# A linear head's norm ahead of its gate, output products taken head by head, and other buffers for half of the token-major weights

## The chip, the core and the metric

The kernel runs on one core of one Trainium2 chip. The core has a matrix engine (TensorE, PE in the rows), a vector engine (VectorE, DVE), an activation engine (ScalarE, ACT), GpSimd (POOL) and SyncE (SP), which issues most of the DMAs. Each engine works through its own list of instructions in a fixed order. The metric is the device time of one execution in microseconds (us), as the median of several runs.

## The reference

One sequence of 512 tokens with 1024 features passes two blocks, all in float32. The first block adds the output product of two mixers and then a gated feed-forward part (width 2816): eight heads of sparse attention (compressed, selected and window keys) and four linear heads with a decaying state. What matters here is the end of a linear head, and the output product over all heads:

```python
hgrn2_mixer(hq, hf, hi, hg, lb, o_gain):
    ...
    o = rms_norm(o, o_gain) * jax.nn.silu(hg.astype(f32)).reshape(B, T, H, dv)
    return o.reshape(B, T, H * dv)

first_block:
    mix = jnp.concatenate([o_nsa.astype(x.dtype), o_hgrn.astype(x.dtype)], axis=-1)
    x = x + mix @ w_out[l]
```

The second block has two layers. Each runs eight heads of stick-breaking attention and four heads of differential attention, adds their output product, and then a feed-forward part of width 4096 with a squared relu:

```python
        df_out = (rmsnorm(df_heads, subln_norm[l]) * (1.0 - lambda_init)).reshape(B, S, DF_WIDTH)
        mixed = jnp.concatenate([sb_out, df_out.astype(sb_out.dtype)], axis=-1)
        x = x + jnp.einsum('bse,ed->bsd', mixed, w_o[l])
```

A final norm follows.

## The kernel before

**Layout.** The sequence lies feature-major: eight tiles X of 128 features x 512 tokens. Every float32 factor of a large product is split into a high and a low part (`_h`, `_l`), and `mm3` (L407) makes one product of three matmuls: high x high, low x high, high x low. A matmul of 128 x 128 weights against 512 tokens is a "weight matmul" below. `load_w` (L383) brings a block of weights: SyncE issues a DMA into a `raw` buffer (3 of them), ScalarE casts the high part (L402) into a slot of the `hi` ring (2 slots), VectorE subtracts to get the low part (L403) in the `lo` ring (2 slots). With `tags` it uses other buffers in place of these rings (`kh`, `kl`), which otherwise hold keys and the compression weights.

**Products.** `gemm_fm` (not shown) makes feature-major results from loaded blocks. `gemm_nat` (L456) makes token-major ones, in four token blocks; it serves `whi` (the values `hv` of the linear heads) and `wvsw`. Results of these go to two PSUM banks (`mm`) and are read from there: `add_residual` adds them to X on VectorE (L504). `gemm_late` (L471) makes an output product of four heads of which the last are not ready when it starts: it waits until three heads are there, does their parts (k = 0, 1, 2) of two output tiles in `mm` banks and, when the scores are through, of more tiles in banks that the scores leave (`wl` in the names); then it waits for the fourth head, adds its part (k = 3) to each, emits them, and does the other tiles by `gemm_fm`. Before, it serves `w_out[0]` (the sparse heads) and, in each layer, `w_o2[l, 1]` (the differential heads). `w_out[1]` (the linear heads) goes through `gemm_fm`.

**Heads.** `hgrn_head` (L650) makes a linear head; its last product is `hpv`, whose squares ScalarE sums (`hsq`, L545). `head_out` (L547) makes the norm: the small `ho_v`, `nr_a`, `ho_rn` instructions on VectorE, the product `ho` (L564), four transposes `ho_t` on PE (L571), then the gate `hs` (L577) and the split in `ho_m_h` and `ho_m_l`. The gate of head h comes from the product `whg` (g0 to g3), through `gx`, `gsg` and `hs`. A differential head goes the same way without a gate: `dfo` (L1385), `dsq`, `do`, `do_t`, `do_m_h`.

**Order.** Several streams are written as Python generators: the linear heads, the setup and the units of the sparse attention, and the dense products (`dense1`). The table `ORDER1` (L39) is the order of the dense stream: i = whi, q = whqf, g = whg, n = sparse projections, v = wvsw, w = an output product, m = wait until that entry of `mix` (4 to 7 are the linear heads) is there. `_drive` (L178) calls the streams in turn and lets each go on when a planner (`Clock`, L73) with cost estimates for every engine and for DMAs (L141) thinks its inputs ready; `until` waits in this planning, not on the chip. Instructions written with `LOOKAHEAD` = 250 (L33) of priority, as the loads in `load_w`, are placed earlier. What comes out is one fixed list for each engine; on the chip an instruction waits in its list until its inputs and its buffer are free, and all behind it wait too.

The second block has its own streams and `ORDER2`; its differential attention and `gemm_late` run side by side there.

## Time and profile before

| what | value |
|---|---|
| median of 3 runs | 1999.33 us (1998.72 to 2000.38) |
| profiled execution: its own time | 1998.82 us |
| its span on the core | 1997.0 us |
| granted TensorE clock, mean | 0.996 of full |
| TensorE busy | 1964.2 us (98%) |
| VectorE busy | 1173.9 us (59%) |
| ScalarE busy | 885.3 us (44%) |
| GpSimd busy | 48.5 us (2%) |
| DMA | 168.65 MB, mean 84 GB/s |

The profiled execution is one run of the program; its span is the part between the first and the last instruction, 1.8 us shorter than its time. A row of a timeline gives the start and the duration of an instruction (or of several alike), then the line, the operation, what it writes and reads, and in brackets how long the engine had been idle before and what released it. Matmuls overlap their neighbours, so the step from one start to the next is shorter than the duration. In the names of rows buffer numbers are left out.

### The profile page before, as it was taken

To read this page: it belongs to the slowest core of one execution; us is meant where nothing else is said; L and a number is where in the kernel's file an instruction comes from. 1 tells how busy PE (TensorE), PEld (TensorE's weight loads), DVE (VectorE), ACT (ScalarE), POOL (GpSimd) and SP (SyncE) were. 2 spreads that over 40 slices of the span, in tenths; PEclk is the share of its full clock that TensorE was granted. 3 is DMA by queue.
4 is the path that set the end of the run, shared out by engine and by line. 5 is a ranking of instruction groups with operands and counts; after the bars stand their busy time and mean duration, and the time that the engine had idled before them with its cause. 6 is when DMAs were issued, how large, how long until landed. Compare 5 with 4: busy or idle time off the path is not lost.

```text
span 1997.0 us, 25958 instructions
## 1 busy us (share of the span) xinstructions
PE 1964.2 (98%) x10197; PEld 1602.2 (80%) x10197; DVE 1173.9 (59%) x2032; ACT 885.3 (44%) x1497; POOL 48.5 (2%) x92
## 2 busy tenths in 40 slices
PE   8999999999999999999999999999999999999998
PEld 7888876788888878787788888888887778888887
DVE  7687777644444455558764444447466864444445
ACT  7656445422222235677542233335487653222233
POOL 1000100000000000000000000000000000000000
PEclk9999999999999999999999999999999999999999
DMA  6222100222222222212222222223221212222222
GB/s 209 69 79 71 48 33 12 74 94 94 94 98 93 94 91 85 85 48 75 72 87 96 95 97 96 97 97 97 79 64 59 85 64 95 95 95 95 96 95 74
DMA packets 50922, 168.65 MB, mean 84 GB/s; under 512 B 5808, under 2 KB 8240, under 8 KB 50800
## 3 DMA queue, kind: packets, MB, share of 16 engines
q1 hardware_dynamic: 47680, 161.93, 24.6%
q0 software_dynamic: 2976, 4.98, 1.2%
q8 instruction: 81, 1.33, 0.3%
q14 instruction: 41, 0.34, 0.1%
q10 hardware_dynamic: 144, 0.07, 0.0%
HBM read 160.14 MB, written 2.10 MB: 81 GB/s over the span
## 4 chain that ended last, share of the span: by engine, by line
PE 89%; ACT 5%; DVE 4%; issue 2%; DMA 1%; SPq 0%; POOL 0%; DVEq 0%; ACTq 0%
PE L0wf_p L410 6%; PE L0wf_p L408 6%; PE L0wf_p L409 6%; PE L1wf_p L408 5%; PE L1wf_p L410 5%; PE L1wf_p L409 5%; PE wgu_p L408 4%; PE wgu_p L410 4%; PE wgu_p L409 4%; PE wdn_p L408 2%; PE wdn_p L410 2%; PE wdn_p L409 2%; PE hpl L710 1%; PE po L1076 1%; PE pt L1057 1%
## 5 line engine op out<-in xcount | busy, mean ns | idle before, releaser
L402 ACT CAST L0wf_h<-L0wf_r 128x1024 fp32r<-128x1024 f32 x64 | 67.3, 1051 | 226.2 <-PE L0wf_p L410 224.8
L402 ACT CAST L1wf_h<-L1wf_r 128x1024 fp32r<-128x1024 f32 x60 | 63.1, 1052 | 218.5 <-PE L1wf_p L410 217.3
L410 PE MATMUL wgu_p<-h_l,wgu_h 128*128 128x512 f32 x328 | 128.8, 393 | 0.0
L408 PE MATMUL wgu_p<-h_h,wgu_h 128*128 128x512 f32 x328 | 128.7, 392 | 0.0
L409 PE MATMUL wgu_p<-h_h,wgu_l 128*128 128x512 f32 x328 | 128.7, 392 | 0.0
L402 ACT CAST wgu_h<-wgu_r 128x1024 fp32r<-128x1024 f32 x44 | 46.2, 1051 | 161.7 <-issue 63.5
L408 PE MATMUL L0wf_p<-L0u_h,L0wf_h 128*128 128x512 f32 x256 | 100.7, 393 | 0.0
L409 PE MATMUL L0wf_p<-L0u_h,L0wf_l 128*128 128x512 f32 x256 | 100.4, 392 | 0.0
L410 PE MATMUL L0wf_p<-L0u_l,L0wf_h 128*128 128x512 f32 x256 | 99.4, 393 | 0.0
L410 PE MATMUL L0wf_p<-L0m_l,L0wf_h 128*128 128x512 f32 x240 | 94.2, 393 | 0.0
L410 PE MATMUL L1wf_p<-L1m_l,L1wf_h 128*128 128x512 f32 x240 | 94.2, 393 | 0.0
L408 PE MATMUL L1wf_p<-L1m_h,L1wf_h 128*128 128x512 f32 x240 | 94.2, 392 | 0.0
L408 PE MATMUL L0wf_p<-L0m_h,L0wf_h 128*128 128x512 f32 x240 | 94.2, 392 | 0.0
L409 PE MATMUL L0wf_p<-L0m_h,L0wf_l 128*128 128x512 f32 x240 | 94.1, 392 | 0.0
L409 PE MATMUL L1wf_p<-L1m_h,L1wf_l 128*128 128x512 f32 x240 | 94.1, 392 | 0.0
L403 DVE TENSOR_TENSOR L0wf_l<-L0wf_r,L0wf_h 128x1024 fp32r<-128x1024 f32 x64 | 78.4, 1225 | 23.4 <-ACT L0wf_h L402 23.4
L408 PE MATMUL L1wf_p<-L1u_h,L1wf_h 128*128 128x512 f32 x224 | 88.6, 395 | 0.0
L409 PE MATMUL L1wf_p<-L1u_h,L1wf_l 128*128 128x512 f32 x224 | 87.9, 392 | 0.0
L410 PE MATMUL L1wf_p<-L1u_l,L1wf_h 128*128 128x512 f32 x224 | 87.1, 394 | 0.0
L403 DVE TENSOR_TENSOR L1wf_l<-L1wf_r,L1wf_h 128x1024 fp32r<-128x1024 f32 x60 | 73.5, 1225 | 22.0 <-ACT L1wf_h L402 22.0
L504 DVE TENSOR_TENSOR X<-X,L0wf_p 128x512 f32<-128x512 f32 x64 | 43.9, 687 | 67.2 <-PE L0wf_p L410 67.2
L504 DVE TENSOR_TENSOR X<-X,L1wf_p 128x512 f32<-128x512 f32 x56 | 38.5, 688 | 67.3 <-PE L1wf_p L410 67.3
(904 smaller groups left out, 5383.8 us busy)
## 6 DMA issues: line engine op xcount, KB each, us to landing
L0wf_r<-w_ff SPq DMA_DIRECT2D x64, 512.0 KB, 3.3
L1wf_r<-w_ff SPq DMA_DIRECT2D x60, 512.0 KB, 3.3
wgu_r<-w_gu SPq DMA_DIRECT2D x44, 512.0 KB, 3.3
wdn_r<-w_dn SPq DMA_DIRECT2D x22, 512.0 KB, 3.3
wns_r<-w_nsa SPq DMA_DIRECT2D x8, 512.0 KB, 3.6
L0wsb_r<-w_sbqk SPq DMA_DIRECT2D x8, 512.0 KB, 3.3
L0wdf_r<-w_dfqk SPq DMA_DIRECT2D x8, 512.0 KB, 3.2
L1wsb_r<-w_sbqk SPq DMA_DIRECT2D x8, 512.0 KB, 3.3
```

The lines of the kernel that those rows point to most:

```text
L402: S.copy(hi[:, c], raw[:, c])
L403: V.tensor_tensor(lo[:, c], raw[:, c], _f(hi)[:, c], ALU.subtract)
L408: TE.matmul(ps, lh, rh, start=start, stop=False)
L409: TE.matmul(ps, ll, rh, start=False, stop=False)
L410: TE.matmul(ps, lh, rl, start=False, stop=stop)
L504: V.tensor_tensor(X[m], X[m], ps, ALU.add)
L710: TE.matmul(pl[:, b * 64 : (b + 1) * 64], ke[:, b * P : (b + 1) * P], qr[:, b * 64 : (b + 1) * 64], start=True, stop=True)
L1057: TE.transpose(pt[:, o + j * P : o + (j + 1) * P], p[g][:, j * P : (j + 1) * P], ident)
L1076: TE.matmul(po[g * 64 : (g + 1) * 64, 0:P], vsw[:, j, br * 128 + g * 64 : br * 128 + (g + 1) * 64], p[g][:, j * P : (j + 1) * P], start=Fa ...
```

## The change

It has five parts. `ORDER1` loses "m7", so that the dense stream goes on to w1 (`w_out[1]`) without a wait for the last linear head. The planner counts a DMA with 0.58 and 3.4 us in place of 0.5 and 3.0; this is an estimate used for ordering only. `gemm_nat` takes `tags` for its second half of weights, and whi passes ("kh", "kl"). `gemm_late` starts when the first head is there in place of three, goes over the heads outside and over its two tiles inside, waiting for each head, works with one block only where there are no scores to wait for, and now serves `w_out[1]` as well. And a linear head no longer waits for its gate before `hpv`: `head_out` takes the gate as a function and asks for it just before the transposes.

```diff
--- before.py
+++ after.py
@@ -36,7 +36,7 @@
 
 
 
-ORDER1 = "i0 q1 g0 n4 i1 q2 n6 g1 n0 m4 n7 n1 g2 m5 q3 n5 n2 n3 v0 g3 m7 w1"
+ORDER1 = "i0 q1 g0 n4 i1 q2 n6 g1 n0 m4 n7 n1 g2 m5 q3 n5 n2 n3 v0 g3 w1"
 
 
 ORDER2 = "q0 q2 s q1 d0 q3 v m3 d1 d2 d3 w0 w1 w3 w2"
@@ -138,7 +138,7 @@
                     if e != eng:
                         start = max(start, t + 0.06)
             if type(x).__name__ == "InstDMACopy":
-                end, eng = self.fit(eng, start, 0.5) + 3.0, "DMA"
+                end, eng = self.fit(eng, start, 0.58) + 3.4, "DMA"
             elif eng == "PE":
                 self.free["PE"] = start + cost
                 end = start + cost + 0.2
@@ -453,10 +453,11 @@
             G.dma_start(kh[o, g], kh[r, g])
         return kh, kl
 
-    def gemm_nat(src, h, emit, name):
+    def gemm_nat(src, h, emit, name, tags=None):
+
 
         cols = src.shape[3]
-        w = [load_w(src[hf], f"{name}_{hf}") for hf in range(2)]
+        w = [load_w(src[hf], f"{name}_{hf}", tags if hf else None) for hf in range(2)]
         for tb in range(NB):
             ps = bank("mm", f"{name}_p{tb}")[:, :cols]
             t = slice(tb * P, (tb + 1) * P)
@@ -474,27 +475,31 @@
 
         tiles = []
         cols = src.shape[3]
-        yield from until(lambda: all(x is not None for x in hs[:3]))
+        yield from until(lambda: hs[0] is not None)
         loaded = [load_w(src[b], f"{name}_{b}") for b in range(2)]
-        for b in range(2):
-            wh, wl = loaded[b]
+        for b in range(1 if scored is None else 2):
+            wh, wl = loaded.pop(0)
             if b == 1:
                 yield from until(scored)
                 loaded = [load_w(src[2], f"{name}_2", ("kh", "kl"))]
                 banks = spare_banks()
+            new = []
             for m in range(cols // P):
-                ps = bank("mm", f"{name}_p{b}_{m}") if b == 0 else banks[m]
                 c = slice(m * P, (m + 1) * P)
-                tiles.append((b * (cols // P) + m, ps, wh[:, 3, c], wl[:, 3, c]))
-                for k in range(3):
-                    mm3(ps, wh[:, k, c], wl[:, k, c], hs[k][0], hs[k][1], k == 0, False)
+                new.append((b * (cols // P) + m, bank("mm", f"{name}_p{b}_{m}") if b == 0 else banks[m], wh[:, :, c], wl[:, :, c]))
+            for k in range(3):
+                yield from until(lambda: hs[k] is not None)
+                for m, ps, wh, wl in new:
+                    mm3(ps, wh[:, k], wl[:, k], hs[k][0], hs[k][1], k == 0, False)
                     yield True
+            tiles += new
         yield from until(lambda: hs[3] is not None)
         for m, ps, wh, wl in tiles:
-            mm3(ps, wh, wl, hs[3][0], hs[3][1], False, True)
+            mm3(ps, wh[:, 3], wl[:, 3], hs[3][0], hs[3][1], False, True)
             emit(m, ps)
             yield True
-        yield from gemm_fm(src[2:], hs, emit, name + "x", 2 * (cols // P), loaded=loaded)
+        b = 1 if scored is None else 2
+        yield from gemm_fm(src[b:], hs, emit, name + "x", b * (cols // P), loaded=loaded)
 
     def run(gen):
         for _ in gen:
@@ -564,6 +569,8 @@
         V.tensor_tensor(o.rearrange("p (b f) -> p b f", f=P), pv.rearrange("p (b f) -> p b f", f=P),
                         rn[:, :, None].to_broadcast([P, NB, P]), ALU.mult)
         yield True
+        if gate is not None:
+            yield from until(lambda: gate() is not None)
         yield from ready(o)
         yield from bank_free("t", banks_of["t"])
         pt = bank("t", name + "_t")
@@ -574,7 +581,7 @@
             S.activation(hi, pt, AF.Copy, scale=gain)
             V.scalar_tensor_tensor(lo, pt, gain, _f(hi), ALU.mult, ALU.subtract)
         else:
-            V.scalar_tensor_tensor(o, pt, gain, gate, ALU.mult, ALU.mult)
+            V.scalar_tensor_tensor(o, pt, gain, gate(), ALU.mult, ALU.mult)
             S.copy(hi, o)
             V.tensor_tensor(lo, o, _f(hi), ALU.subtract)
         yield True
@@ -752,7 +759,7 @@
             V.copy_predicated(at, lev_mask[:, 1792:2304], pd)
             yield True
 
-            yield from until(lambda: hv[NB - 1] is not None, lambda: hs[h] is not None)
+            yield from until(lambda: hv[NB - 1] is not None)
             yield from ready(at, at0, at1, hv[NB - 1])
             yield from bank_free("o", 1)
             pv = bank("o", f"hpv{h}")
@@ -769,7 +776,7 @@
                     TE.matmul(pv[:, q_], a, v_, start=(i == 0), stop=(i == b))
                 head_squares(pv, f"hsq{h}_{b}", ss, b)
             yield True
-            mix[4 + h] = yield from head_out(pv, ss, C["o_gain"], hs[h], f"ho{h}")
+            mix[4 + h] = yield from head_out(pv, ss, C["o_gain"], lambda: hs[h], f"ho{h}")
 
         def hgrn_all():
             for h in range(4):
@@ -1117,7 +1124,7 @@
                     if g == 1:
                         hv[tb] = tiles[tb]
 
-                yield from gemm_nat(d["w_hi"][g], h1, emit_hv, f"whi{g}")
+                yield from gemm_nat(d["w_hi"][g], h1, emit_hv, f"whi{g}", ("kh", "kl"))
 
             def vsw_():
                 yield from gemm_nat(d["w_vsw"], h1, emit_vsw, "wvsw")
@@ -1141,7 +1148,7 @@
                 elif k == "m":
                     yield from until(lambda: mix[n] is not None)
                 elif k == "w":
-                    yield from gemm_fm(d["w_out"][n], mix[4 * n : 4 * n + 4], add_residual, f"wout{n}")
+                    yield from gemm_late(d["w_out"][n], Late(mix, 4 * n), add_residual, f"wout{n}", None, None)
             yield from gemm_late(d["w_out"][0], Late(mix, 0), add_residual, "wout0", lambda: "scored" in comp,
                                  lambda: [bank("s", f"wl{i}") for i in range(2)])
 
```

How the lists of instructions change is shown at three places.

**ScalarE, near the start.** `whi` is the first product of the dense stream (i0), `whqf_0` and `whqf_1` are the blocks of the second (q1); `hv` are the four results of whi, `hsg` and `hx` belong to a linear head. Before:

```order
L402 CAST whi_1_h<-whi_1_r 128x1024
L1116 ACTIVATE hv_347<-whi_p_363,st_rn 128x256
L350 COPY st_rb<-st_pb 128x512
L1116 ACTIVATE hv_348<-whi_p_389,st_rn 128x256
L627 ACT_TABLE_LOAD
L627 ACTIVATE hsg_275<-hx_273 128x512
L627 ACTIVATE hsg_311<-hx_309 128x512
L377 ACT_TABLE_LOAD
L402 CAST whqf_0_h<-whqf_0_r 128x1024
L637 ACTIVATE hx_309<-hsg_311,lbg,oml 128x512
L402 CAST whqf_1_h<-whqf_1_r 128x1024
L1116 ACTIVATE hv_349<-whi_p_427,st_rn 128x256
```

And with the change:

```order
L611 ACTIVATE lbe<-lbe 128x8
L402 CAST whqf_0_h<-whqf_0_r 128x1024
L1123 ACTIVATE hv_347<-whi_p_363,st_rn 128x256
L1123 ACTIVATE hv_348<-whi_p_389,st_rn 128x256
L350 COPY st_rb<-st_pb 128x512
L634 ACT_TABLE_LOAD
L634 ACTIVATE hsg_275<-hx_273 128x512
L634 ACTIVATE hsg_311<-hx_309 128x512
L377 ACT_TABLE_LOAD
L402 CAST whqf_1_h<-whqf_1_r 128x1024
L644 ACTIVATE hx_309<-hsg_311,lbg,oml 128x512
L1123 ACTIVATE hv_349<-whi_p_427,st_rn 128x256
```

The second half of whi goes to `whi_1kh` (its cast is the row ahead of this piece), and the cast of whqf_0 stands before the first `hv` in place of after the two `hsg`; the cast of whqf_1 is the only one between the table load and the third `hv`.

**VectorE and PE, after the norm of linear head 3.** `sc` are the scores of the compressed keys, `nm`, `sm` and `p` belong to the softmax of the window and selected keys, X_96 and X_97 are the first two tiles of X, `wout_1` and `wout1x` (`wout_2` before) are the later blocks of `w_out[1]`. VectorE before:

```order
L1027 TENSOR_REDUCE nm_2440<-s_1_2447 128x1
L1041 TENSOR_SCALAR p_2422<-p_2422,sm_2410 128x256
L579 TENSOR_TENSOR ho_m_l<-ho_2278,ho_m_h 128x512
L1041 TENSOR_SCALAR p_2422<-p_2422,sm_2410 128x256
L1029 TENSOR_TENSOR nm_2440<-nm_2440,rq 128x2
L504 TENSOR_TENSOR X_96<-X_96,wout_p_0_2351 128x512
L504 TENSOR_TENSOR X_97<-X_97,wout_p_1_2398 128x512
L540 COPY p_2371<-pt_0_2405 128x256
L403 TENSOR_TENSOR wout_2_l<-wout_2_r,wout_2_h 128x1024
```

VectorE with the change:

```order
L584 SCALAR_TENSOR_TENSOR ho_2233<-ho_t,packed,hs_2278 128x512
L988 TENSOR_REDUCE cm<-sc 128x32
L586 TENSOR_TENSOR ho_m_l<-ho_2233,ho_m_h 128x512
L989 TENSOR_TENSOR sc<-sc,cm 128x1024
L1034 TENSOR_REDUCE nm_2338<-s_0_2340 128x1
L1034 TENSOR_REDUCE nm_2338<-s_1_2345 128x1
L1034 TENSOR_REDUCE nm_2368<-s_0_2370 128x1
L403 TENSOR_TENSOR wout1x_l<-wout1x_r,wout1x_h 128x1024
L1036 TENSOR_TENSOR nm_2338<-nm_2338,rq 128x2
L509 TENSOR_TENSOR X_96<-X_96,wout_p_0_2306 128x512
L509 TENSOR_TENSOR X_97<-X_97,wout_p_1_2307 128x512
```

And PE with the change, from the last head's part of the two tiles on:

```order
L408 MATMUL wout_p_0_2306<-ho_m_h,wout_0_h 128x512
L409 MATMUL wout_p_0_2306<-ho_m_h,wout_0_l 128x512
L408 MATMUL wout_p_1_2307<-ho_m_h,wout_0_h 128x512
L409 MATMUL wout_p_1_2307<-ho_m_h,wout_0_l 128x512
L410 MATMUL wout_p_0_2306<-ho_m_l,wout_0_h 128x512
L410 MATMUL wout_p_1_2307<-ho_m_l,wout_0_h 128x512
L408 MATMUL wout1x_p_0_2429<-ho_m_h,wout_1_h 128x512
L409 MATMUL wout1x_p_0_2429<-ho_m_h,wout_1_l 128x512
L410 MATMUL wout1x_p_0_2429<-ho_m_l,wout_1_h 128x512
```

Before, the addition to X_96 stands ahead of the low part of the next block of weights; now the low part `wout1x_l` stands ahead of it, with a cast on ScalarE before that, into the slot that block `wout_0` holds. On PE the two tiles of `w_out[1]` now end one right after the other, and the next matmul uses the bank of the first.

**PE, at the end of layer 0's differential attention.** `dfo` is the last head's last product, `do3_t` its transposes, `do0` to `do2` are the heads before it; the numbers in the names are those of heads and tiles. Before (five more weight matmuls of the same kind stand between the last dfo and the first row here):

```order
L410 MATMUL L0wl_8642<-L0do2_m_l_8513,L0wo1_1_h_8580 128x512
L408 MATMUL L0wl_8642<-L0do0_m_h_7926,L0wo1_1_h_8580 128x512
L409 MATMUL L0wl_8642<-L0do0_m_h_7926,L0wo1_1_l_8581 128x512
L410 MATMUL L0wl_8642<-L0do0_m_l_7927,L0wo1_1_h_8580 128x512
L408 MATMUL L0wl_8642<-L0do1_m_h_8351,L0wo1_1_h_8580 128x512
L409 MATMUL L0wl_8642<-L0do1_m_h_8351,L0wo1_1_l_8581 128x512
L410 MATMUL L0wl_8642<-L0do1_m_l_8352,L0wo1_1_h_8580 128x512
L408 MATMUL L0wl_8642<-L0do2_m_h_8512,L0wo1_1_h_8580 128x512
L571 MATMUL L0do3_t_8646<-packed_82,L0do3_8628 128x128 x4
L409 MATMUL L0wl_8642<-L0do2_m_h_8512,L0wo1_1_l_8581 128x512
L410 MATMUL L0wl_8642<-L0do2_m_l_8513,L0wo1_1_h_8580 128x512
L408 MATMUL L0wo1_p0_0_8585<-L0do3_m_h_8651,L0wo1_0_h_8574 128x512
```

And with the change:

```order
L408 MATMUL L0wl_8622<-L0do2_m_h_8526,L0wo1_1_h_8567 128x512
L1392 MATMUL L0dfo3_8530<-L0dv0_7184,L0dp15_8545 128x128
L1392 MATMUL L0dfo3_8530<-L0dv1_7185,L0dp15_8545 128x128
L1392 MATMUL L0dfo3_8530<-L0dv2_7186,L0dp15_8545 128x128
L1392 MATMUL L0dfo3_8530<-L0dv3_7187,L0dp15_8545 128x128
L409 MATMUL L0wl_8622<-L0do2_m_h_8526,L0wo1_1_l_8568 128x512
L410 MATMUL L0wl_8622<-L0do2_m_l_8527,L0wo1_1_h_8567 128x512
L578 MATMUL L0do3_t_8655<-packed_82,L0do3_8644 128x128 x4
L408 MATMUL L0wo1_p0_0_8572<-L0do3_m_h_8660,L0wo1_0_h_8561 128x512
```

Thirteen weight matmuls stood between the last dfo and `do3_t`, and two between it and the first matmul that uses the last head; now there are two and none. Layer 1 has the same pattern. Outside these places and the stretches that lead to them, the first block's attention and the differential attention among them, the lists are the same.

## Rows read from the trace of the kernel before

**Rows 1.** The page's part 1: the span, and TensorE's busy time and share.
```profile
span 1997.0 us, 25958 instructions
...
PE 1964.2 (98%) x10197; PEld 1602.2 (80%) x10197; DVE 1173.9 (59%) x2032; ACT 885.3 (44%) x1497; POOL 48.5 (2%) x92
```

**Rows 2.** The page's part 4: the chain that ended last, shares by engine.
```profile
PE 89%; ACT 5%; DVE 4%; issue 2%; DMA 1%; SPq 0%; POOL 0%; DVEq 0%; ACTq 0%
```

**Rows 3.** Timeline of PE, end of layer 0's differential attention (start, duration, ..., [idle before <-releaser]).
```profile
990.14 1.13 PE L1385 MATMUL L0dfo<-L0dv,L0dp 128*128 128x128 f32 x8
991.02 0.48 PE L408 MATMUL L0wl<-L0do_m_h,L0wo_h 128*128 128x512 f32 x1
...
993.89 0.39 PE L408 MATMUL L0wl<-L0do_m_h,L0wo_h 128*128 128x512 f32 x1
994.46 0.63 PE L571 MATMUL L0do_t<-packed,L0do 128*128 128x128 f32 x4 [0.19 <-DVE L0do L564]
994.85 0.47 PE L409 MATMUL L0wl<-L0do_m_h,L0wo_l 128*128 128x512 f32 x1
...
995.87 0.50 PE L408 MATMUL L0wo_p<-L0do_m_h,L0wo_h 128*128 128x512 f32 x1 [0.32 <-ACT L0do_m_h L574]
```

**Rows 4.** Timeline of PE, the first whqf matmul after whi.
```profile
34.73 0.50 PE L408 MATMUL whqf_p<-h_h,whqf_h 128*128 128x512 f32 x1 [1.71 <-ACT hv L1116]
```

**Rows 5.** Timeline of ScalarE, ahead of that matmul.
```profile
31.61 1.05 ACT L402 CAST whqf_h<-whqf_r 128x1024 fp32r<-128x1024 f32 x1
...
34.21 0.47 ACT L1116 ACTIVATE hv<-whi_p,st_rn 128x256 f32<-128x256 f32 x1
```

**Rows 6.** Timeline of PE around the norm of linear head 3.
```profile
227.46 1.87 PE L970 MATMUL cs<-kcT,nq 128*128 128x32 f32 x16
...
229.53 0.36 PE L1024 MATMUL s<-nk0h,nq 128*128 128x256 f32 x1
...
229.88 0.48 PE L408 MATMUL wout_p<-ho_m_h,wout_h 128*128 128x512 f32 x1
...
234.61 1.07 PE L769 MATMUL hpv<-hv,at 128*128 128x128 f32 x8
...
238.03 0.38 PE L1024 MATMUL s<-nk0h,nq 128*128 128x256 f32 x1 [0.88 <-ACT p L1036]
...
243.35 1.11 PE L571 MATMUL ho_t<-packed,ho 128*128 128x128 f32 x4 [3.88 <-DVE ho L564]
```

**Rows 7.** Busy PE by stretch: stretch, us, PE busy (instructions), granted clock, DMA share, GB/s.
```profile
30.00:36.00 6.00, 4.29 (x32) 1.00 0.18 31
240.00:241.00 1.00, 0.00 (x0) 0.87 0.00 0
243.00:247.00 4.00, 3.65 (x15) 0.50 0.00 0
247.00:248.00 1.00, 1.00 (x8) 0.71 0.00 0
```

**Rows 8.** Timelines of ScalarE, then VectorE, behind head 3: cast, X additions, low part.
```profile
249.20 1.06 ACT L402 CAST wout_h<-wout_r 128x1024 fp32r<-128x1024 f32 x1
...
247.80 0.69 DVE L504 TENSOR_TENSOR X<-X,wout_p 128x512 f32<-128x512 f32 x1 [0.66 <-PE wout_p L410]
248.93 0.69 DVE L504 TENSOR_TENSOR X<-X,wout_p 128x512 f32<-128x512 f32 x1 [0.44 <-PE wout_p L410]
...
250.29 1.23 DVE L403 TENSOR_TENSOR wout_l<-wout_r,wout_h 128x1024 fp32r<-128x1024 f32 x1 [0.34 <-ACT wout_h L402]
```

**Rows 9.** Busy PE by stretch: block 1's attention, layer 0's attention.
```profile
312.00:354.00 42.00, 39.81 (x305) 1.00 0.08 26
900.00:950.00 50.00, 48.83 (x263) 1.00 0.23 69
```

**Rows 10.** Timeline of PE, end of layer 1's differential attention.
```profile
1611.71 0.63 PE L571 MATMUL L1do_t<-packed,L1do 128*128 128x128 f32 x4 [0.23 <-DVE L1do L564]
...
1613.12 0.50 PE L408 MATMUL L1wo_p<-L1do_m_h,L1wo_h 128*128 128x512 f32 x1 [0.31 <-ACT L1do_m_h L574]
```

## The prediction

> **What bounds the kernel now.** I read the page's busy shares first: TensorE is busy for 1964.2 of 1997.0 us [rows 1], so 32.8 us of idle time are all that an order can win, beside the clock. The chain that ended last agrees: PE is 89% of it [rows 2]. VectorE and ScalarE count only where PE stands behind them. So I went through PE's timeline for its idle stretches and then looked, in the order of the changed program, at which of them have other work in front of them. A weight matmul (128x512) is worth one step from start to start: 13 of them stand between 991.02 and 993.89, 12 steps in 2.87 us, 0.24 each [rows 3]. Three places change: the start (near 34 us), the norm of linear head 3 (near 240 us), and the end of the differential attention in each of the two layers (near 994 and 1612 us). All sums are made against the profiled execution, 1998.82 us; the median shown, 1999.33, lies 0.51 above it, and I add that at the end. A measurement of this kernel can tell about 0.2% (4.0 us) from no change.
>
> **The change, part by part.**
>
> *A, weights of whi in kh/kl (gemm_nat).* PE waits 1.71 us before its first whqf matmul, for the third hv that ScalarE writes [rows 4]; ScalarE had the cast of whqf_0 in front of it, from 31.61, and wrote hv only at 34.21 [rows 5]. With whi's second half in other buffers a slot of the hi ring is free earlier, and the order shows the whqf_0 cast moved to before the first hv. So one cast of 1.05 us less stands in front of the third hv; the other cast and a table load stay there. The wait shrinks by about that cast: **-1.0 us**. Ends: -1.71 (all of it) and 0 (VectorE, which has whqf's low parts to make, gives it back). On SP's queue the loads of the compression weights, which use kh too, move behind whi; they are needed much later, cost nothing, and if they were late the compression would show it.
>
> *B, head 3 and w_out[1].* Now: whg ends near 227.46, the last 8 of hpv's 20 matmuls run from 234.61, then PE does attention rows until the norm lets ho_t start at 243.35, after waits of 0.88 and **3.88 us** [rows 6]. And the clock falls: 0.50 of full (1.2 GHz) over 243 to 247 and 0.71 in the next microsecond [rows 7], where 3.65 us of busy time at half and 1.00 at 0.71 did 0.5 x 3.65 + 0.29 = 2.1 us less work.
> In the changed order hpv (20 matmuls; the last 8 took 1.07 with their drain, so 0.11 to 0.13 each) stands among whg's, so whg ends some 2.2 us later, near 229.6, the norm runs beside it, and ho_t needs no wait. Behind whg PE has 24 weight matmuls (24 x 0.24 = 5.8), two groups of 8 cs (16 take 1.7 without their drain), three score units (229.53 to 229.88, 0.35 each) [rows 6] and ho_t (0.4, as do_t takes from 994.46 to 994.85 [rows 3]): 9.0 us, until 238.6. Then stands the first wout1x matmul. Its bank is free when VectorE has added X_96, and X_96 stands behind the low part wout1x_l, that behind its cast, and the cast's slot is given back by the very matmul ahead, at about 238.9. Cast 1.06, low part 1.23, add 0.69 [rows 8] and handoffs: PE resumes near 242.2. So a hole of 3.88 + 0.88 becomes one of about 3.2, at another place. Against before: 243.35 - 242.2 = 1.2 us sooner, with 6 weight matmuls and ho_t more done and four score units fewer: 1.4 + 0.4 - 1.4 = 0.4. That is -1.6. If the clock falls after this hole as it did after the old one, that is all; if it does not, another -2.1. I take **-2.6**, since the new hole is shorter; ends -1.6 and -3.7.
> A rule weighed here: in the trace of before the two wout_p tiles end one after the other, their X additions at 247.80 and 248.93 [rows 8], with matmuls between. The Trainium skill, Perfetto Trace Analysis, section Matmuls, says that groups of matmuls should rotate through banks so that one's evacuation overlaps the next one's matmuls; the new gemm_late ends both tiles together, with nothing left to rotate to, and by the addition alone (0.69) the wait would be some 0.8 us and B -4.0, by the chain above 3.2 and -1.6, both before the clock.
>
> *C, the rest of block 1's attention.* The w_out[1] matmuls that stood between score units are used up sooner; PE's holes in 312 to 354 come to 42.00 - 39.81 = 2.2 us [rows 9]. With less filler I take **+0.7**, ends 0 and +1.5. The dropped "m7" has no cost of its own: gemm_late waits for its heads itself.
>
> *D, the end of the differential attention, both layers.* Here gemm_late now starts with the first head in place of the third, so its matmuls are used earlier. Before: from the last dfo (990.14, 8 matmuls, until about 991.02) the norm takes until do_t at 994.46, and PE fills it with 13 weight matmuls, the first at 991.02, and idles 0.19; then two more (994.85) cover part of the 1.41 us until do_m_h lets k=3 start at 995.87, idle 0.32 [rows 3]. In the changed order 2 stand in front of do_t and none behind it. The norm's chain depends on PE's dfo alone and stays as long. 15 - 2 = 13 matmuls no longer cover it: 13 x 0.24 = **3.1 us** in each layer; seen as holes, some 2.7 at do_t and 0.8 at k=3. Layer 1 has the same pattern, 0.23 and 0.31 idle now [rows 10]. **+6.2 us** for both.
> Could the matmuls moved forward pay there? Only if PE waited there, and in 900 to 950 it is idle for 50.00 - 48.83 = 1.2 us [rows 9]: I take -0.15 per layer, **-0.3**, ends -1.2 and 0 each.
>
> *E, the clock at these ends.* The trace has no hole there to show it. Bounds from the nearest rows: after the wait of 1.71 the clock stayed at 1.00 [rows 4, 7], so 0; the wait of 3.88 cost 2.1 [rows 7]. The new holes (2.7 and 0.8 with little between) lie between: **+1.0** per layer, **+2.0**, ends 0 and +4.2.
>
> *F, the planner's DMA cost* (0.58 and 3.4 for 0.5 and 3.0) issues nothing; the order outside these places, stick-breaking and both feed-forward parts, is the same: 0.
>
> Sum: -1.0 - 2.6 + 0.7 + 6.2 - 0.3 + 2.0 = **+5.0 us**: 2003.8 for the profiled execution, **2004.3** on the scale of the median.
>
> **Rivals.**
> 1. *Faster.* The filler closes more than it opens. Its place is head 3: if ScalarE gets the wout1x cast done while PE is still in whg's delayed matmuls or the X additions go ahead, no hole remains (-0.88 - 3.88 - 2.1 = -6.9), the start gives its whole 1.7, and of the layers' 6.2 the 2.4 of D's end come back in the earlier waits: -6.9 - 1.7 + 6.2 - 2.4 = -4.8, **1994.5**. It decides from the point where less than about 1 us of idle is left before the first wout1x matmul. For it: idle in the layers' earlier waits exists [rows 9]. Against: the order fixes the cast behind the last w_out matmul.
> 2. *No change.* The clock holds at both ends (E = 0) and after the new hole (B = -3.7): -1.0 - 3.7 + 0.7 + 6.2 - 0.3 = +1.9, **2001.2**. For it: the clock still averaged 0.87 over 240 to 241, well inside the old hole [rows 7], and a wait of 1.71 left no mark. Against: the old hole did bring it down.
> 3. *The clock falls at every new hole.* B = -1.6, E = +4.2: -1.0 - 1.6 + 0.7 + 6.2 - 0.3 + 4.2 = +8.2, **2007.5**. For it: at 243 to 247 us it stood at half for some microseconds after work had resumed [rows 7]. The Trainium skill, TensorE: Matmul & The Clock Gate, section "Loop structure matters more than you think", speaks against this change: it calls for a loop that runs all k of an output tile back to back, and says that a long wait inside it takes the engine to its lower clock; the new loop puts its wait between the k.
>
> **How the numbers follow.** The order is fixed and shows D plainly, so the forecast (+5.0) gets 0.45, its own range 2002 to 2008; rival 1 0.16, rival 2 0.22, rival 3 0.17. The range of 8 in 10 leaves out half of rival 1 and the upper part of rival 3: **1995.5 to 2008.5**. Slower by over 0.2% means above 2003.3: three quarters of the forecast and rival 3, 0.51. Faster, below 1995.3: rival 1 for the most part, 0.15. Within 0.2%: 0.34.
>
> **What would show it.** Right: PE idle of 2.5 to 3 us before L0do_t and L1do_t and 0.7 to 0.9 before the following wo_p; ho_t without a wait; a new wait of about 3 us before the first wout1x matmul, behind X; the wait before whqf at about 0.8. Wrong: do_t still covered, or a hole in the scores of block 1 of many microseconds; the clock's rows of 240 to 250, 990 to 1002 and 1608 to 1620 tell rivals 2 and 3 apart.

## The result, and the profile of the changed kernel

The changed kernel is slower: a median of 2011.07 us (4 runs, 2008.74 to 2011.38) against 1999.61 us (4 runs), a ratio of 1.0055 with a 95% interval of 1.0043 to 1.0067. That is +11.5 us; +5.0 was forecast, and 2008.5 was the upper end of the range. Run a second time, beside other kernels (changed_third below), it took 2007.60 us against 2000.27, a ratio of 1.0043 (1.0029 to 1.0057). The direction holds; the two sizes differ by 4.2 us, and the profiles show most of that in the clock (below). Five single executions of 2138.97 to 6859.89 us (one each of planner_only, late_undone_in_layers, heads_only and the kernel before, and the only one of changed_again) are left out of every median and ratio here.

The page of the profiled execution (2011.26 us), part 1, to be read against [rows 1]:

```profile
span 2009.5 us, 25946 instructions
...
PE 1971.0 (98%) x10197; PEld 1609.4 (80%) x10197; DVE 1178.4 (59%) x2032; ACT 884.6 (44%) x1497; POOL 49.3 (2%) x92
```

TensorE is busy 6.8 us longer with the same 10197 instructions and the same sizes. So part of the loss is not waiting: the same matmuls took longer.

**Where the time went.** Three pairs of rows lay the two executions side by side. They are answers about one tile: line, operation and count, then shortest/median/longest duration, and the start of the first and the last of them. First the kernel before (layer 0's and layer 1's stick-breaking scores, layer 1's feed-forward part):

```profile
L1302 PE MATMUL L0z<-L0sh,tri_r x80: 274/337/499, 778.7 to 901.4; 128*128 128x256 f32 x32, 128*128 128x384 f32 x32, 128*128 128x512 f32 x16
...
L1302 PE MATMUL L1z<-L1sh,tri_r x80: 274/338/497, 1395.9 to 1518.5; 128*128 128x256 f32 x32, 128*128 128x384 f32 x32, 128*128 128x512 f32 x16
...
L408 PE MATMUL L1wf_p<-L1m_h,L1wf_h x240: 389/390/404, 1639.6 to 1960.3; 128*128 128x512 f32 x120
```

And the changed kernel:

```profile
L1309 PE MATMUL L0z<-L0sh,tri_r x80: 274/338/497, 781.2 to 903.9; 128*128 128x256 f32 x32, 128*128 128x384 f32 x32, 128*128 128x512 f32 x16
...
L1309 PE MATMUL L1z<-L1sh,tri_r x80: 274/338/496, 1403.4 to 1526.0; 128*128 128x256 f32 x32, 128*128 128x384 f32 x32, 128*128 128x512 f32 x16
...
L408 PE MATMUL L1wf_p<-L1m_h,L1wf_h x240: 389/390/405, 1651.8 to 1972.5; 128*128 128x512 f32 x120
```

The changed kernel is 2.5 us late at the start of layer 0 (781.2 against 778.7), 7.5 us at that of layer 1, and 12.2 us at the feed-forward part of layer 1. Block 1 lost 2.5 us, layer 0 5.0 and layer 1's attention 4.7. The places are those of the prediction; the sizes aren't.

PE's timeline at the end of layer 0's differential attention, and the two rows of layer 1, against [rows 3, 10]:

```profile
995.08 1.13 PE L1392 MATMUL L0dfo<-L0dv,L0dp 128*128 128x128 f32 x8
995.97 0.48 PE L409 MATMUL L0wl<-L0do_m_h,L0wo_l 128*128 128x512 f32 x1
996.28 0.39 PE L410 MATMUL L0wl<-L0do_m_l,L0wo_h 128*128 128x512 f32 x1
999.40 0.63 PE L578 MATMUL L0do_t<-packed,L0do 128*128 128x128 f32 x4 [2.73 <-DVE L0do L569]
1000.81 0.79 PE L408 MATMUL L0wo_p<-L0do_m_h,L0wo_h 128*128 128x512 f32 x1 [0.78 <-ACT L0do_m_h L581]
...
1621.57 1.09 PE L578 MATMUL L1do_t<-packed,L1do 128*128 128x128 f32 x4 [2.72 <-DVE L1do L569]
1623.43 0.80 PE L408 MATMUL L1wo_p<-L1do_m_h,L1wo_h 128*128 128x512 f32 x1 [0.78 <-ACT L1do_m_h L581]
```

Two weight matmuls follow the last dfo, then PE waits 2.73 us for do_t (0.19 before), and 0.78 us for the first matmul of k=3 (0.32 before). Layer 1 shows 2.72 and 0.78. These are the holes that the prediction gave as 2.7 and 0.8. From the last dfo to k=3 it takes 5.73 us in both kernels (990.14 to 995.87 [rows 3], 995.08 to 1000.81): the norm's chain is as long as before, and the loss is that the last dfo itself comes 2.4 us later in the layer, with 13 more weight matmuls ahead of it.

The granted clock by stretch (stretch, us, PE busy (instructions), clock, DMA share, GB/s), against [rows 7]:

```profile
194.00:195.00 1.00, 1.00 (x8) 0.68 0.89 360
195.00:197.00 2.00, 2.00 (x10) 0.50 0.06 21
197.00:198.00 1.00, 1.00 (x8) 0.61 0.00 0
242.00:244.00 2.00, 1.30 (x3) 0.54 0.51 135
244.00:248.00 4.00, 4.00 (x13) 0.50 0.16 64
248.00:250.00 2.00, 2.00 (x11) 0.76 0.00 0
1000.00:1002.00 2.00, 1.22 (x4) 0.50 0.03 8
1002.00:1006.00 4.00, 4.00 (x11) 0.50 0.00 0
1006.00:1008.00 2.00, 2.00 (x8) 0.82 0.46 119
1621.00:1623.00 2.00, 1.09 (x4) 0.53 0.00 0
1623.00:1627.00 4.00, 3.56 (x8) 0.50 0.00 0
1627.00:1629.00 2.00, 2.00 (x8) 0.76 0.00 0
```

Ahead of the final norm the clock falls four times, in place of once. Each time the work done at half speed (1.2 GHz) is what counts: near 194 us 0.32 + 2 x 0.5 + 0.39 = 1.7 us lost, near 244 us 1.30 x 0.46 + 4 x 0.5 + 2 x 0.24 = 3.1 us (2.1 in the one fall before), behind do_t in layer 0 1.22 x 0.5 + 4 x 0.5 + 2 x 0.18 = 3.0 us, in layer 1 1.09 x 0.47 + 3.56 x 0.5 + 2 x 0.24 = 2.8 us. That is 10.6 us of lost work against 2.1. Where waits follow, a part of it is made up: PE is busy 6.8 us longer, so somewhat more than half of the 12.5 us by which the span grew is the clock. Most of the rest is the later last dfo, 2.4 us in each layer.

Head 3: PE's wait, and the chain that ends it (PE, then ScalarE, then VectorE):

```profile
239.01 0.63 PE L410 MATMUL wout_p<-ho_m_l,wout_h 128*128 128x512 f32 x2
242.70 0.80 PE L408 MATMUL wout1x_p<-ho_m_h,wout_h 128*128 128x512 f32 x1 [3.06 <-DVE X L509]
...
239.68 1.04 ACT L402 CAST wout1x_h<-wout1x_r 128x1024 fp32r<-128x1024 f32 x1 [2.12 <-PE wout_p L410]
...
240.75 1.23 DVE L403 TENSOR_TENSOR wout1x_l<-wout1x_r,wout1x_h 128x1024 fp32r<-128x1024 f32 x1 [0.39 <-ACT wout1x_h L402]
241.90 0.15 DVE L1036 TENSOR_TENSOR nm<-nm,rq 128x2 f32<-128x2 f32 x1
241.97 1.28 DVE L509 TENSOR_TENSOR X<-X,wout_p 128x512 f32<-128x512 f32 x2
```

This is the chain of term B. The cast of wout1x waits for the slot of the last w_out matmul, the low part follows, then the X addition, and PE resumes at 242.70 after 3.06 us (242.2 and 3.2 were forecast).

The first whqf matmul, against [rows 4]:

```profile
34.28 0.50 PE L408 MATMUL whqf_p<-h_h,whqf_h 128*128 128x512 f32 x1 [0.88 <-ACT hv L1123]
```

The wait fell from 1.71 to 0.88 us, as forecast; the first matmul is only 0.45 us earlier than at 34.73, because stages ahead of it were a little later.

### The profile page after: what moved, and what is told of

Read it like the earlier page. It is cut to its first block, busy times and chain, and to the rows that moved or that the text cites. A ratio compares the mean times of both kernels' runs of the same rounds, so it can differ in the third digit from the quotient of the medians.

```text
span 2009.5 us, 25946 instructions
## 1 busy us (share of the span) xinstructions
PE 1971.0 (98%) x10197; PEld 1609.4 (80%) x10197; DVE 1178.4 (59%) x2032; ACT 884.6 (44%) x1497; POOL 49.3 (2%) x92
## 4 chain that ended last, share of the span: by engine, by line
PE 88%; ACT 5%; DVE 4%; issue 1%; DMA 1%; SPq 0%; POOL 0%; DVEq 0%; ACTq 0%
PE L0wf_p L410 6%; PE L0wf_p L408 6%; PE L0wf_p L409 6%; PE L1wf_p L408 5%; PE L1wf_p L410 5%; PE L1wf_p L409 5%; PE wgu_p L410 4%; PE wgu_p L409 4%; PE wgu_p L408 4%; PE wdn_p L408 2%; PE wdn_p L410 2%; PE wdn_p L409 2%; PE hpl L717 1%; PE pt L1064 1%; PE po L1083 1%
```

## The experiments

Two theories were set against each other. Theory 1: the planner's DMA figures, which the prediction costed at nothing, move the weight matmuls away from the last head's norm in the layers. Theory 2, that of the prediction: gemm_late does it, by starting with the first head.

**planner_only: the kernel before with the planner's figures alone.**

```diff
-                end, eng = self.fit(eng, start, 0.5) + 3.0, "DMA"
+                end, eng = self.fit(eng, start, 0.58) + 3.4, "DMA"
```

> The kernel before with one edit: the planner counts a DMA with 0.58 and 3.4 in place of 0.5 and 3.0. Theory 1 (the planner's DMA figure moves the weight matmuls away from the last head's norm in both layers, and the waits there then bring the clock down): in the new PE order 4 weight matmuls stand between the last dfo and do_t and none behind it, so 11 of 15 lose their place, 11 x 0.24 = 2.6 us a layer, and the clock costs some 2.4 a layer as in the changed kernel: about +10 us, 2009.5, with block 1 as before up to 400 us. Theory 2 (the reasoning of the prediction: gemm_late's earlier start does it, and the planner's figure costs nothing): 1999.6, no change.

Measured: 2006.90 us against 1999.35, ratio 1.0039 (1.0026 to 1.0052): +7.6 us, where theory 1 gave about +10. Its PE timeline in both layers (idle of 2.26 and 0.78 us):

```profile
996.78 0.63 PE L571 MATMUL L0do_t<-packed,L0do 128*128 128x128 f32 x4 [2.26 <-DVE L0do L564]
998.18 0.79 PE L408 MATMUL L0wo_p<-L0do_m_h,L0wo_h 128*128 128x512 f32 x1 [0.78 <-ACT L0do_m_h L574]
...
1617.49 0.63 PE L571 MATMUL L1do_t<-packed,L1do 128*128 128x128 f32 x4 [2.26 <-DVE L1do L564]
1618.90 0.69 PE L408 MATMUL L1wo_p<-L1do_m_h,L1wo_h 128*128 128x512 f32 x1 [0.78 <-ACT L1do_m_h L574]
```

Theory 2 has nothing to say to this: gemm_late is untouched here, and the holes are there. With the new gemm_late the hole at do_t grows from 2.26 to 2.73 us, since two matmuls in place of four stand in front of it; that is its share. PE's list shows how it begins. `L0ds` is the score of differential head 1, which reads keys `L0dk1h` whose second half a DMA on GpSimd brings (L453). Before, the list goes from the first row below to the score at once; with the new figures six more weight matmuls stand between (the first and the last of them are shown):

```
L410 MATMUL L0wdf_p_0_7936<-L0h_l,L0wdf_1_h 128x512
L408 MATMUL L0wdf_p_0_8023<-L0h_h,L0wdf_0_h 128x512
...
L410 MATMUL L0wdf_p_0_8023<-L0h_l,L0wdf_0_h 128x512
L1346 MATMUL L0ds_8032<-L0dk1h,L0dq_7781 128x384
```

The planner takes the keys for later, lets the dense stream go ahead, and all weight matmuls behind it come earlier in the list; at the end of the stream they are missing. With 3.4 alone and 0.5 kept, PE's list comes out the same as with both figures, so 0.58 has no part in it. That it is this DMA was read from the list; no run changed it alone.

**planner_undone: the changed kernel with the old figures.**

```diff
-                end, eng = self.fit(eng, start, 0.58) + 3.4, "DMA"
+                end, eng = self.fit(eng, start, 0.5) + 3.0, "DMA"
```

> The changed kernel with the planner's DMA figures put back to 0.5 and 3.0, all else as changed. Theory 1: 13 and 2 weight matmuls stand around do_t again, do_t waits about 0.2 us, and what is left is block 1: +0.5 to +3 us on before, 2000 to 2002.5. Theory 2: still about 2009 to 2011, since gemm_late still starts with the first head.

Measured: 1998.99 us against 1999.35, ratio 1.0000 (0.9991 to 1.0010). Its tail in layer 0:

```profile
993.86 0.63 PE L578 MATMUL L0do_t<-packed,L0do 128*128 128x128 f32 x4 [0.17 <-DVE L0do L569]
...
995.26 0.50 PE L408 MATMUL L0wo_p<-L0do_m_h,L0wo_h 128*128 128x512 f32 x1 [0.31 <-ACT L0do_m_h L581]
```

The holes are back to 0.17 and 0.31 us though gemm_late starts with the first head. The whole loss hangs on a number that issues no instruction.

**late_undone_in_layers: the changed kernel with the old gemm_late in the layers.**

```diff
-            yield from gemm_late(d["w_o2"][l, 1], Late(mixed, 4), add_residual, L + "wo1", lambda: "scored" in st, last_banks)
+            yield from gemm_late_old(d["w_o2"][l, 1], Late(mixed, 4), add_residual, L + "wo1", lambda: "scored" in st, last_banks)
```

Here `gemm_late_old` is the function of the kernel before.

> The changed kernel with the old gemm_late (waits for three heads, tile by tile) for the output product of the layers alone. Theory 1: hardly better than the changed kernel, since 4 matmuls in place of 2 stand in front of do_t and none behind: 2009.5 to 2011. Theory 2: the layers are as before, some 9.5 us come back: 2001.5.

Measured: 2007.76 us against 1999.35, ratio 1.0040 (1.0026 to 1.0054), which can't be told from the changed kernel (1.0055 and 1.0043); theory 1 gave 2009.5 to 2011. do_t still waits, 2.87 us in layer 0 (from the last dfo to do_t it took 4.93 us there, in place of 4.32), and in layer 1:

```profile
1619.80 0.63 PE L606 MATMUL L1do_t<-packed,L1do 128*128 128x128 f32 x4 [2.26 <-DVE L1do L597]
1621.21 0.51 PE L408 MATMUL L1wo_p<-L1do_m_h,L1wo_h 128*128 128x512 f32 x1 [0.78 <-ACT L1do_m_h L609]
```

**late_only_in_layers: the reverse, the new gemm_late for the layers in the kernel before.**

```diff
-            yield from gemm_late(d["w_o2"][l, 1], Late(mixed, 4), add_residual, L + "wo1", lambda: "scored" in st, last_banks)
+            yield from gemm_late_new(d["w_o2"][l, 1], Late(mixed, 4), add_residual, L + "wo1", lambda: "scored" in st, last_banks)
```

> The kernel before with the new gemm_late for the output product of the layers alone. Theory 1 (the planner's figure moves the matmuls): 13 and 2 matmuls stay around do_t, 1999.4, no change. Theory 2 (gemm_late's earlier start): +9.5 us, 2009.

Measured: 2000.05 us against 2000.27, ratio 1.0001 (0.9992 to 1.0010). Theory 2 falls on both sides.

**tail_filled: what the clock costs there.** The changed kernel with ten matmuls in front of the last head's transposes; what they write is overwritten by the transposes.

```diff
         pt = bank("t", name + "_t")
+        if name.endswith("do3"):
+            for _ in range(10):
+                TE.matmul(pt, identb, masks, start=True, stop=True)
```

> The changed kernel with 10 bf16 matmuls of the constant masks (128x512, into the bank that the transposes then overwrite) in front of the last head's do_t in each layer: no useful work, only to fill the 2.7 us wait. If idle time is what brings the clock down behind do_t (rows of the changed kernel: 0.50 over some 6 us, worth 2.5 us a layer), the clock stays at 1.00 there and the time falls by about 5 us to 2006. If the clock falls whatever PE does there, or the filling delays do_t, 2011 to 2012.

Measured: 2005.54 us against 1999.35, ratio 1.0029 (1.0017 to 1.0041). Its timeline and the clock behind do_t in both layers:

```profile
994.14 2.32 PE L579 MATMUL L0do_t<-masks 128*128 128x512 bf16 x10
...
997.41 0.66 PE L581 MATMUL L0do_t<-packed,L0do 128*128 128x128 f32 x4 [0.49 <-DVE L0do L569]
998.84 0.50 PE L408 MATMUL L0wo_p<-L0do_m_h,L0wo_h 128*128 128x512 f32 x1 [0.78 <-ACT L0do_m_h L584]
...
1000.00:1006.00 6.00, 6.00 (x28) 1.00 0.27 89
1618.00:1624.00 6.00, 5.62 (x24) 1.00 0.11 16
```

do_t comes hardly earlier after the last dfo than in the changed kernel (4.24 us against 4.32), and nothing useful is done in the filled time, but the clock stays at 1.00 where it stood at 0.50. From the first k=3 matmul to the first wo1x matmul layer 0 takes 1001.1 - 998.84 = 2.3 us here, 1004.8 - 1000.81 = 4.0 in the changed kernel and 998.1 - 995.87 = 2.2 before (first starts of wo1x from the answers about that tile). So the idle stretch in front of do_t is what brings the clock down, and the second, of 0.78, did not do it alone. The other profiles agree: the clock fell behind do_t in all eight ends with a wait of 2.26 us or more in front of it (both layers of the changed kernel, changed_third, planner_only and late_undone_in_layers), and in none of the fourteen where do_t waited about 0.2. What is left (+6.2 us) is for the most part the later last dfo, 2 x 2.4 us. By the medians the filling can't be told from changed_third (1.0043, with overlapping intervals); its effect is read from these rows.

**whi_buffers_only.**

```diff
-                yield from gemm_nat(d["w_hi"][g], h1, emit_hv, f"whi{g}")
+                yield from gemm_nat(d["w_hi"][g], h1, emit_hv, f"whi{g}", ("kh", "kl"))
```

> The kernel before with one edit: whi's second half of weights in the kh/kl buffers. By the profile of the changed kernel the wait before the first whqf matmul falls from 1.71 to some 0.9 us and a start of 0.4 us earlier is left at 190 us; nothing else moves. Theory 1: -0.4 us, 1999.0, the same within the measurement. If the clock falls near 194 us, as it did in the changed kernel after waits of 0.34 and 0.75 that the kernel before has too, +1.3 us, 2000.7; that would tie this fall to when the waits come, not to how long they are.

Measured: 1999.52 us against 1999.57, ratio 1.0000 (0.9991 to 1.0009). The wait is 0.88 us as in the changed kernel, and the first whqf matmul comes 0.44 us earlier than before, at 34.29. In its profile the clock fell near 194 us (0.91 over 180 to 200 us).

**heads_only: norm ahead of the gate and w_out[1] through gemm_late, in the kernel before.** The edit is the change's own in `hgrn_head`, `head_out`, `ORDER1` and the "w" branch of `dense1`; the layers keep the old function.

> The kernel before with the linear head's norm ahead of the gate and w_out[1] through the new gemm_late (no m7), nothing else. Theory 1: ho_t without a wait, a wait of 3.1 us before the first wout1x matmul in place of 0.88 and 3.88 (-1.7), and some 1.5 us more of waits in 280 to 360 us, where the weight matmuls are missing: about 0, 1999.4, with up to 2 us less or 1 us more by whether the clock falls after that wait. Rival (the gain of the prediction, with C at 0.7): -1 to -3 us, 1996.5 to 1998.5.

Measured: 1999.74 us against 1999.57, ratio 1.0000 (0.9991 to 1.0010). One row of 3.06 us stands in place of [rows 6]'s two, ho_t waits for nothing, and the waits in the attention grow: in the changed kernel they come to 3.57 us from the first wout1x matmul to 362 us (3.97 in this run), against 2.05 us before from ho_t on (the waits of that stretch added up). What the head gains (0.88 + 3.88 - 3.06 = 1.7 us of waits) is spent there.

**x_before_weights: planner_undone with the X additions ahead of the low part.**

```diff
             mm3(ps, wh[:, 3], wl[:, 3], hs[3][0], hs[3][1], False, True)
-            emit(m, ps)
+            if scored is None:
+                clock.take()
+                with tc.high_priority(offset=250):
+                    emit(m, ps)
+            else:
+                emit(m, ps)
```

> The changed kernel with the planner's figures put back, and the additions to X_96 and X_97 placed ahead of the low part wout1x_l on VectorE. If that low part and its cast are what the first wout1x matmul waits for (its bank, by X_96), the wait falls from 3.06 to about 1 us and the time by 2 us to 1997; if another wait stands behind it (the softmax behind the low part, or the weights), the wait only moves on and it stays at 1999.

Measured: 1997.17 us against 1999.57, ratio 0.9987 (0.9978 to 0.9997): faster than both kernels. PE's wait before the first wout1x matmul:

```profile
239.99 0.50 PE L408 MATMUL wout1x_p<-ho_m_h,wout_h 128*128 128x512 f32 x1 [0.78 <-DVE X L514]
```

It fell from 3.06 to 0.78 us. So the addition behind a cast and a low part was the wait. Against planner_undone, which differs by this edit alone, the gain is 2.0 us (-2.4 and -0.4, each against the kernel before in its own series). **heads_and_x** is heads_only with the same edit, so without whi's buffers:

> The kernel before with the head part (norm ahead of the gate, w_out[1] through the new gemm_late) and the X additions ahead of wout1x_l, without whi's buffers and with the planner's old figures. If the X order is what gains, 1997 to 1997.7 (0.4 us more at the start than with the buffers); if the buffers are needed too, 1999.4.

Measured: 1996.93 us against 2000.27, ratio 0.9985 (0.9975 to 0.9994), the lowest median of the study, though not to be told from x_before_weights. whi's buffers aren't needed for it.

**changed_again and changed_third: the changed kernel unchanged, for its clock.**

> The changed kernel once more, unchanged, for the clock alone. If the falls of the clock in block 1 come with the list of instructions, it shows 0.91 in 180 to 200 us and 0.83 in 240 to 260 us again; if they depend on when the waits fall, one of them can be missing or shorter, while the two behind do_t, after longer waits, stay.

Its one execution took 6859.89 us and doesn't answer the question, so the kernel was run again.

> The changed kernel again, unchanged, beside the two below, for its clock: 2011 us, and behind do_t in both layers the clock at 0.50 for some 6 us. If the falls in block 1 depend on when the waits come, 180 to 200 us and 240 to 260 us show other values than 0.91 and 0.83; if they belong to the list, the same.

Measured: 2007.60 us against 2000.27, ratio 1.0043 (1.0029 to 1.0057). The rows that answer to those of the changed kernel above, the starts of the layers last:

```profile
194.00:198.00 4.00, 4.00 (x33) 1.00 0.26 102
242.00:250.00 8.00, 8.00 (x46) 1.00 0.14 56
996.00:998.00 2.00, 1.22 (x7) 0.91 0.00 0
998.00:1000.00 2.00, 2.00 (x6) 0.50 0.00 0
1000.00:1002.00 2.00, 2.00 (x8) 0.74 0.00 0
...
241.39 0.50 PE L408 MATMUL wout1x_p<-ho_m_h,wout_h 128*128 128x512 f32 x1 [3.06 <-DVE X L509]
...
995.71 0.63 PE L578 MATMUL L0do_t<-packed,L0do 128*128 128x128 f32 x4 [2.73 <-DVE L0do L569]
997.11 0.50 PE L408 MATMUL L0wo_p<-L0do_m_h,L0wo_h 128*128 128x512 f32 x1 [0.78 <-ACT L0do_m_h L581]
...
L1309 PE MATMUL L0z<-L0sh,tri_r x80: 274/338/497, 777.3 to 900.0; 128*128 128x256 f32 x32, 128*128 128x384 f32 x32, 128*128 128x512 f32 x16
...
L1309 PE MATMUL L1z<-L1sh,tri_r x80: 274/338/504, 1398.7 to 1521.4; 128*128 128x256 f32 x32, 128*128 128x384 f32 x32, 128*128 128x512 f32 x16
...
L408 PE MATMUL L1wf_p<-L1m_h,L1wf_h x240: 389/390/404, 1646.4 to 1967.2; 128*128 128x512 f32 x120
```

The list is the same, the waits are the same (3.06 before wout1x, 2.73 and 0.78 behind dfo), and the clock is not: near 194 and near 242 us it didn't fall at all, and behind do_t it cost 2.00 x 0.5 + 2.00 x 0.26 + 1.22 x 0.09 = 1.6 us in layer 0 in place of 3.0. The five executions of this series run from 2005.91 us to 2009.47, the longer ones at the lower mean clocks (0.997 to 0.994); the four of the first series all stood at 0.993. The later series ran on different chips, and that of the first isn't known, so a part of what lies between the two may belong to the chip; no run separates that. planner_undone, too, has the wait of 3.06 without a fall behind it.

## Why the prediction was wrong, point by point

The two profiles of the changed kernel, laid out by the starts of the layers, of do_t and of the feed-forward part of layer 1 (us against the profile before):

| part | forecast | first profile | changed_third |
|---|---|---|---|
| block 1: A, B, C and the clock there | -2.9 | +2.5 | -1.4 |
| D: do_t later within its layer, both layers | +5.9 | +4.8 | +5.2 |
| E: from do_t on, both layers | +2.0 | +4.9 | +3.0 |
| sum | +5.0 | +12.2 | +6.8 |

**F, the step that failed.** The prediction put the planner's DMA cost at 0, since it "issues nothing". It does issue nothing, and without it there is no loss: planner_undone came out at 1998.99 us. I looked for the cause of the missing matmuls in the code that makes them (gemm_late) and not among all the parts that feed the planner. The list showed the effect rightly; which part did it could have been found without a chip, by building each part alone and laying its list beside that of the kernel before. Had F been right, D would have stood under it with the same price: the number was missed in block 1 and in E.

**D, the holes.** Right in place and kind, wrong in cause. 2.73 and 0.78 us were measured where 2.7 and 0.8 stood in the text. As time it is 2.4 us a layer (k=3 of layer 0 starts 4.9 us late, of which 2.5 were there at the start of the layer), where 3.1 was taken. The 13 matmuls that went ahead thus cost some 0.19 us each in place of 0.24. Waits that they fill are not the reason: PE's waits from the start of layer 0 to the last dfo come to 1.97 us, and to 1.84 before. What the reason is stays open.

**E, the mis-sized term.** +2.0 us was taken with ends at 0 and 4.2; it measured 3.0 and 2.8 us of lost work in the first profile, some 1.6 in layer 0 in changed_third; as time 4.9 and 3.0 us for both layers. The upper bound was the one fall that the trace of before shows (2.1 us each), which was a single sample and no bound: what a fall costs is the work that PE has to do while it lasts, and in the first profile it lasted longer (0.50 from 1000 to 1006 us, in changed_third from 998 to 1000). Rival 3 (+8.2) came nearest: +11.5 us in one series and +7.3 in the other. In the first profile the clock fell at every new hole, and near 194 us too, which no rival had; in changed_third it fell in the layers and not behind head 3.

**B, head 3.** The mechanism was right row by row: whg's end, ho_t without a wait, 3.06 us before wout1x, 242.70 against 242.2. Its price hung on the clock. In the first profile the clock fell behind the new hole and cost 3.1 in place of 2.1 us; of the six profiles with this hole it fell in four and not in two.

**C, mis-sized.** +0.7 was taken; the waits of the attention grew by 1.5 us (2.05 to 3.57), the upper end given.

**A.** -1.0 was taken; the wait shrank by 0.83, the start by 0.4, and in whi_buffers_only the gain couldn't be measured.

So A, B and C together are worth -0.4 us by the medians (planner_undone, not to be told from 0) where -2.9 stood. The first series came out 6.5 us above the forecast; its profile shows that in block 1, where the clock fell twice, and in E. The rule of the Trainium skill weighed in B (Perfetto Trace Analysis, section Matmuls: rotate through banks) held as a direction: where the next matmul had to use the bank of the first tile, it waited for that bank's addition. The larger price by the chain was right: the addition of 0.69 us was a wait of 3.06, since a cast and a low part stood in front of it. The rule of the Trainium skill in rival 3 (TensorE: Matmul & The Clock Gate, section "Loop structure matters more than you think") names a long wait inside the loop, there for a DMA; the runs show that the wait mattered, but not that the loop's order did, since the old loop (late_undone_in_layers) waits about as long (2.87 and 2.26 us).

## What to carry to other kernels

A number in a planner is an edit to the order of every stage that it plans: build each part of a change alone and compare lists before costing any part at nothing. Filler work that is used early is missing where a serial chain ends a stage; look at what stands behind the last product of such a chain. And before a matmul that waits for its bank, look at what stands ahead of the evacuation in its engine's list: moving two additions ahead of a low part was worth 2.0 us here.

## What the hardware showed that was not expected

The clock's falls are not fixed by the list of instructions. With the same waits of 0.34 and 0.75 us near 188 and 192 us the mean clock over 180 to 200 us was 0.91 in the profiles of the changed kernel, planner_undone, whi_buffers_only, late_undone_in_layers, late_only_in_layers and heads_and_x, and 1.00 in those of before, planner_only, heads_only, tail_filled, x_before_weights and changed_third; the product that ends the second wait starts at 191.94 in late_only_in_layers, where the clock fell, and at 191.97 in planner_only, where it didn't. With the same wait of 3.06 us before wout1x the mean over 240 to 260 us was 0.83 (changed), 0.91 (heads_only, tail_filled, late_undone_in_layers) and 1.00 (planner_undone, changed_third). At 8 to 12 us the clock stood at 0.57 to 0.60 in changed_third, planner_only, tail_filled and heads_only, and at 1.00 in the other eight; none of the four is among the six with the fall near 194 us. The longer holes are steadier: the old hole of head 3 (3.87 to 3.89 us) brought the clock down in all four profiles that have it (0.83), the holes at do_t in all eight ends. So one execution of a kernel with such waits can differ from the next by the 3.6 us that the executions of changed_third span, and a fall seen once in a trace is one draw. What decides it stays open.
